# Value projections with 512 moving columns: four of six column groups of a three-block transformer stack

## The chip, the cores and the metric

One NeuronCore of one Trainium2 chip. The metric is the device time of one execution in microseconds, the median over runs; each execution takes some 2.2 ms. A core has a matrix engine (TensorE, PE in the profile; its weight loads are a row of their own, PEld), VectorE (DVE), ScalarE (ACT), GpSimd (POOL) and SyncE (SP), which here issues the weight loads from memory. The engines run their own lists of instructions in order and wait for each other by semaphores.

## What is computed

512 tokens of 1024 features go through a first block (a mixer that joins a four-head mLSTM and a gated convolution, then a feed-forward network) and two more layers (forgetting attention with 16 heads, then HGRN2 with 8 heads, each with its feed-forward network). Three projections matter here, those that make the values of the three mixers:

```
# first block                                   # second block, layer 0 (fox) and layer 1 (hgrn)
proj = u @ w_in                                 proj = einsum('bsd,de->bse', h, w_in)
qk_raw, v, o_pre, gates, glu = split(proj)      q, k, v, f_logit = split(proj)
qk = silu(causal_dwconv(qk_raw))                out = softmax(q k^T / 8 + c_q - c_k) v
q, k = split(qk)                                q, f_logit, i_val, g = split(proj)   # i_val: the values
h = mlstm_chunkwise(q, k, v, gates)             scores = q_t k_s decay(t, s);  o = scores v + ...
```

Each value projection is [512 tokens, 1024 features] times [1024, 1024]. All products are in float32 precision: an operand is split into a high and a low part, and a product is three matmuls (high by high, high by low, low by high), which accumulate in one PSUM bank.

## The kernel before

Activations lie feature-major in `U`, 8 blocks of [128 features, 512 tokens], each as a pair of high and low part. Weights come in units of 128 x 1024 numbers. Class `Weights` holds them in the order of use (the list `names` in `run`, L1683 to L1712): `load` (L145) has SP fetch a unit, `split` makes the high part on ACT (L155) and the low part on DVE (L157), and `take` hands a unit out. Three raw buffers and four of each part exist.

A product is made in one of two ways. `unit` (L440) makes 128 output features for all 512 tokens: the weights are the stationary operand, the tokens the 512 moving columns, 24 matmuls (8 k-blocks of three, L430 to L432). `unit_tok` (L452) makes values, which have to lie token-major: for each of four token blocks a 128 x 128 piece of `U` is stationary and 256 columns of weights move, 24 matmuls (L456 to L458) into one bank of half its width. So a `unit_tok` is 96 matmuls and takes two weight units at once. Both take their banks from `mm`, a ring of four; the side work has another ring of four, `ax`.

The order of PE and SP is the order of the code. Between pieces of the main stream stands `slot` (L387): it emits evacuations that are due (`post`, with a lag of one slot: a result is read out one slot after its last matmul) and then advances the side chains, generators that emit their next step at each slot (`ml_head`, `fox_pair`, `hgrn_head`, norms). A `unit` has a slot after k-blocks 2, 5 and 7, so after 9, 9 and 6 matmuls; a `unit_tok` has eight, one after every 12. ACT and DVE are ordered by a scheduler, which fills gaps of DVE with work of low priority (the 31-tap convolution, L838). `side(gen)` queues a chain; at most `maxside` run at a time, the next one starts when one ends, and `rate` is the number of steps per slot.

The three places:

- mLSTM (`first`, L897 to L907): for each head four `unit`s for q and k, each read out by `ev_qk` (ACT L879, three DVE operations L881, then the silu on ACT L883), then `unit_tok` for the head's 256 value columns, then `side(ml_head(h))`, then two `unit`s for the output gate. `ml_head` makes a broadcast of a gate row (PE L644 and L645), four exponentials of it (ACT L1036), the scores (PE L1045, two matmuls per token block, over the two halves of q and k), and at the end the product with the values (PE L1075).
- Forgetting attention (`fox`, L1320): a `unit_tok` before every other pair of heads, `fox_pair` as the side chain.
- HGRN2 (`hgrn`, L1548): a `unit_tok` after heads 0, 2 and 4 and one near the end; `hgrn_head` is the side chain. Its last steps are the product with the values (PE L1663 to L1667), the square (ACT L1670), the sums over features (PE L562), the power (POOL L567), the broadcast (PE L575), its copy (ACT L1677), two products on DVE (L1679, L1680) and the split into `O[h]` (ACT L599, DVE L600). `proj_out` (L1244) then multiplies all `O` with the output weights: `group` goes through the heads and emits slots until `O[k]` is there.

Of the kernel before, what the change touches and what calls it, by code (L numbers as in the profile page):

```python
# [42 lines left out]
def cols(v):  # L43
    """(..., C) with features along the last axis -> (128, ... * C/128)."""
    v = np.asarray(v)
    v = v.reshape(-1, v.shape[-1] // 128, 128)
    return np.ascontiguousarray(v.transpose(2, 0, 1)).reshape(128, -1)


def units(w, starts):  # L50
    """Column blocks of 128 of w (K, N): (len, 128, K)."""
# [5 lines left out]
def units_tok(w, start):  # L57
    """1024 columns of w (1024, N) as units of 256 columns and 4 k-blocks: (8, 128, 1024)."""
# [4 lines left out]
    return np.ascontiguousarray(np.concatenate(u))  # L63

# [5 lines left out]
def layout(inp):  # L70
# [30 lines left out]
    out["wv"] = units_tok(w, 2048)  # L101
# [16 lines left out]
    out["wfv"] = units_tok(w, 2048)  # L118
# [4 lines left out]
    out["whv"] = units_tok(w, 2048)  # L123
# [5 lines left out]
class Weights:  # L129
    """All weight units in the order of their use: loads and hi/lo splits run ahead of take()."""  # L130
# [30 lines left out]
    def take_blocks(self, tag):  # L161
        """A unit split into blocks of another tag."""
# [21 lines left out]
class Blocks:  # L184
    """A weight unit in two tiles."""
# [8 lines left out]
class Out:  # L194
    """The output of a phase: blocks y and the sums of their squares."""
# [14 lines left out]
class Norm:  # L210
    """x += rms(out) * g, then the blocks of x * gn, split; their norm r is applied later (box)."""
# [61 lines left out]
class ModNorm:  # L273
    """x += rms(out) * g, then the blocks of rms(x) * gain + shift, split."""
# [53 lines left out]
class Final:  # L328
    """x += rms(out) * g, stored."""
# [19 lines left out]
class Kernel:  # L349
# [39 lines left out]
    def slot(self):  # L389
        """Between two pieces of the main stream: due evacuations, side chains, fillers."""  # L390
# [15 lines left out]
    def fill(self, gen, late=1000000):  # L406
        """Work for idle engines."""
# [26 lines left out]
    def unit(self, U, evac, lag=1):  # L434
        """A block of 128 outputs, feature-major; evac(psum [128, T])."""
# [10 lines left out]
    def unit_tok(self, U, evac, lag=1, ax=0):  # L446
        """A block of 256 outputs, token-major; evac(tb, psum [128, 256])."""
# [15 lines left out]

    def group(self, n, get, evacs, kb=KB, ahead=1):
        """n units side by side, one k-block after the other as get(k) hands out its parts."""
# [11 lines left out]
    def group_halves(self, norm, evacs, extra=None, tag="Q"):  # L477
        """The first units of a phase, a half of the tokens after the other, as the norm hands out its blocks."""
# [24 lines left out]
    def tail(self, F, out, evac, nxt, done=4):  # L503
        """The last units of a phase, a half of the tokens after the other; each starts its part of the next norm."""
# [1002 lines left out]
    def hgrn(self, norm, nxt):  # L1507
# [42 lines left out]
        for h in range(6):  # L1550
# [3 lines left out]
            if h % 2 == 0:  # L1554
                self.unit_tok(U, ev_v(h // 2))
# [197 lines left out]
```

## Time and profile before

| what | value |
|---|---|
| three runs | 2204.05, 2207.32, 2210.89 us; median 2207.32 |
| profiled execution | span 2204.7 us from first to last instruction; its own time is not listed, only the span |
| granted TensorE clock, mean | 0.991 |
| PE busy | 2151.4 us, 98% of the span |
| PEld, DVE, ACT busy | 84%, 63%, 42% |
| weight traffic | 209 MB, 95 GB/s on average |

Busy PE does not mean PE at its peak: the ends of matmuls are modelled, and a matmul's record is longer than the distance to the next one's start. How fast PE goes is read from the distance between starts. Idle time of an engine that is not the bottleneck costs nothing.

### The profile page before, as it was taken

To read this page: it belongs to the slowest core of one execution; us is meant where nothing else is said; L and a number is where in the kernel's file an instruction comes from. 1 tells how busy PE (TensorE), PEld (TensorE's weight loads), DVE (VectorE), ACT (ScalarE), POOL (GpSimd) and SP (SyncE) were. 2 spreads that over 40 slices of the span, in tenths; PEclk is the share of its full clock that TensorE was granted. 3 is DMA by queue.
4 is the path that set the end of the run, shared out by engine and by line. 5 is a ranking of instruction groups with operands and counts; after the bars stand their busy time and mean duration, and the time that the engine had idled before them with its cause. 6 is when DMAs were issued, how large, how long until landed. Compare 5 with 4: busy or idle time off the path is not lost.

```text
span 2204.7 us, 30667 instructions
## 1 busy us (share of the span) xinstructions
PE 2151.4 (98%) x12224; PEld 1850.0 (84%) x12224; DVE 1395.6 (63%) x2391; ACT 917.8 (42%) x1485; POOL 52.8 (2%) x81
## 2 busy tenths in 40 slices
PE   7999999989999999999999999999999999999997
PEld 5788888888888889888898888888899889888887
DVE  4799999977455557755565243458787837434445
ACT  4434433555333334655543222236566544232221
POOL 0000000000000000000000000000000000000000
PEclk9999999999999999999999999999999999999999
DMA  8332224613422331212113223222211112232321
GB/s 293 106 134 77 68 68 134 230 58 127 141 95 89 105 94 56 71 58 67 59 58 117 100 94 100 93 89 88 77 49 58 49 58 96 87 105 89 103 91 62
DMA packets 67966, 209.01 MB, mean 95 GB/s; under 512 B 7664, under 2 KB 9840, under 8 KB 67824
## 3 DMA queue, kind: packets, MB, share of 16 engines
q1 hardware_dynamic: 67824, 207.06, 28.0%
q8 instruction: 96, 1.57, 0.3%
q14 instruction: 46, 0.38, 0.1%
HBM read 204.94 MB, written 2.10 MB: 94 GB/s over the span
## 4 chain that ended last, share of the span: by engine, by line
PE 71%; DVE 3%; ACT 2%; issue 1%; POOL 0%; DMA 0%; POOLq 0%; DVEq 0%; ACTq 0%
PE mm L430 19%; PE mm L431 19%; PE mm L432 19%; PE ax L1606 2%; PE mm L456 1%; PE mm L457 1%; PE mm L458 1%; PE ax L1435 1%; PE ax L1412 1%; DVE wl L157 1%; PE ax L562 1%; PE ax L432 1%; PE ax L430 1%; PE ax L431 1%; PE ax L1379 0%
## 5 line engine op out<-in xcount | busy, mean ns | idle before, releaser
L430 PE MATMUL mm<-U,wh 128*128 128x512 f32 (+1 forms) x1768 | 672.1, 380 | 4.1 <-ACT U L319 3.0
L432 PE MATMUL mm<-U,wl 128*128 128x512 f32 (+1 forms) x1768 | 657.8, 372 | 2.0 <-DVE wl L157 2.0
L431 PE MATMUL mm<-U,wh 128*128 128x512 f32 (+1 forms) x1768 | 657.4, 372 | 1.8 <-DVE U L320 1.8
L155 ACT CAST wh<-w 128x1024 fp32r<-128x1024 f32 (+1 forms) x325 | 335.6, 1035 | 748.0 <-PE mm L431 458.6
L157 DVE TENSOR_TENSOR wl<-w,wh 128x1024 fp32r<-128x1024 f32 (+1 forms) x325 | 389.8, 1202 | 208.5 <-ACT wh L155 185.0
L430 PEld LDWEIGHTS mm<-U,wh 128*128 128x128 f32 x1768 | 336.1, 190 | 65.0 <-issue 3.9
L432 PEld LDWEIGHTS mm<-U,wl 128*128 128x128 f32 x1768 | 335.4, 190 | 60.6 <-DVE wl L157 2.6
L431 PEld LDWEIGHTS mm<-U,wh 128*128 128x128 f32 x1768 | 335.9, 190 | 56.8 <-DVE U L320 2.3
L430 PE MATMUL mm<-H,wh 128*128 128x512 f32 (+1 forms) x868 | 309.2, 356 | 0.7 <-ACT H L599 0.7
L431 PE MATMUL mm<-H,wh 128*128 128x512 f32 (+1 forms) x868 | 306.5, 353 | 0.2 <-DVE H L600 0.2
L432 PE MATMUL mm<-H,wl 128*128 128x512 f32 (+1 forms) x868 | 306.5, 353 | 0.0
L430 PEld LDWEIGHTS mm<-H,wh 128*128 128x128 f32 x868 | 164.2, 189 | 23.3 <-ACT H L599 0.9
L432 PEld LDWEIGHTS mm<-H,wl 128*128 128x128 f32 x868 | 164.1, 189 | 22.8 <-DVE wl L157 0.2
L431 PEld LDWEIGHTS mm<-H,wh 128*128 128x128 f32 x868 | 164.2, 189 | 22.6 <-DVE H L600 0.5
L838 DVE SCALAR_TENSOR_TENSOR Y<-G,par,Y 128x505 f32<-128x505 f32 (+26 forms) x240 | 164.6, 729 | 0.5
L456 PE MATMUL mm<-wh,U 128*128 128x256 f32 x368 | 106.9, 291 | 0.0
L458 PE MATMUL mm<-wh,U 128*128 128x256 f32 x368 | 104.6, 284 | 0.0
L457 PE MATMUL mm<-wl,U 128*128 128x256 f32 x368 | 104.5, 284 | 0.0
L1203 DVE TENSOR_TENSOR Y<-Y,mm 128x512 f32<-128x512 f32 (+1 forms) x60 | 34.7, 580 | 106.6 <-PE mm L432 106.4
L1193 DVE TENSOR_TENSOR t<-t,mm 128x512 f32<-128x512 f32 x42 | 28.7, 686 | 102.0 <-PE mm L432 102.0
L1183 DVE TENSOR_TENSOR t<-mm,rb 128x512 f32<-128x512 f32 x42 | 29.0, 690 | 100.9 <-PE mm L432 100.9
L594 DVE TENSOR_TENSOR ss<-ss,t 128x256 f32<-128x256 f32 (+1 forms) x148 | 68.1, 466 | 29.3 <-ACT t L593 29.0
(364 smaller groups left out, 2747.7 us busy)
## 6 DMA issues: line engine op xcount, KB each, us to landing
w<-in_upa SPq DMA_DIRECT2D x44, 512.0 KB, 3.3
w<-in_upb SPq DMA_DIRECT2D x44, 512.0 KB, 3.2
w<-in_upc SPq DMA_DIRECT2D x44, 512.0 KB, 3.2
H<-in_ada SPq DMA_DIRECT2D x48, 256.0 KB, 6.0
w<-in_wglu SPq DMA_DIRECT2D x16, 512.0 KB, 3.8
w<-in_wqk SPq DMA_DIRECT2D x16, 512.0 KB, 3.3
U<-in_ada SPq DMA_DIRECT2D x32, 256.0 KB, 6.5
w<-in_wfqk SPq DMA_DIRECT2D x16, 512.0 KB, 3.3
```

Of the source, the lines that this page charges most:

```text
L155: nc.scalar.copy(wh, raw)
L157: k.V.tensor_sub(wl, raw, wh.bitcast(F32))
L430: mm(ps, lh, rh, start=start, stop=False)
L431: mm(ps, lh, rl, start=False, stop=False)
L432: mm(ps, ll, rh, start=False, stop=stop)
L456: mm(ps, lh, wh[:, k % 4], start=k == 0, stop=False)
L457: mm(ps, lh, wl[:, k % 4], start=False, stop=False)
L458: mm(ps, ll, wh[:, k % 4], start=False, stop=k == 7)
L594: self.V.tensor_add(ss, ss, sq)
L838: self.V.scalar_tensor_tensor(y[:, s:], G[j][:, :T - s], cvw[:, w:w + 1], y[:, s:], op0=ALU.mult, op1=ALU.add)
L1203: self.V.tensor_add(acc[m][:, c], acc[m][:, c], ps[:, c])
L1606: mm(ps[:, ts], W[:, ts], W[:, ts], start=True, stop=True)
```

## The change

A new function makes 512 value columns at a time. It takes four banks at once, one per token block, goes through the k-blocks outside (a weight unit is now 2 k-blocks of 512 columns) and through the token blocks inside, 6 matmuls of 512 moving columns each. After token blocks 0, 1 and 3 it has a slot.

```diff
+    def unit_wide(self, U, evac, lag=1):
+        mm = self.PE.matmul
+        pss = [self.mm() for _ in range(4)]
+        for u in range(4):
+            wh, wl = self.W.take(512)
+            for tb in range(4):
+                ts = slice(tb * 128, (tb + 1) * 128)
+                ps = pss[tb]
+                for k in (2 * u, 2 * u + 1):
+                    lh, ll = U[k][0][:, ts], U[k][1][:, ts]
+                    mm(ps, lh, wh[:, k % 2], start=k == 0, stop=False)
+                    mm(ps, lh, wl[:, k % 2], start=False, stop=False)
+                    mm(ps, ll, wh[:, k % 2], start=False, stop=k == 7)
+                if u == 3:
+                    self.post(lambda tb=tb, ps=ps: evac(tb, ps), lag)
+                if tb != 2:
+                    self.slot()
...
         def ev_v(h):
             def f(tb, ps):
-                nc.scalar.copy(V[tb][h // 2][:, (h % 2) * 256:(h % 2) * 256 + 256], ps)
+                nc.scalar.copy(V[tb][h // 2], ps)
+                if tb == 3:
+                    vdone.add(h // 2)
...
-            self.unit_tok(U, ev_v(h))
-            self.side(self.ml_head(h, qk, V, tho, H))
+            self.side(self.ml_head(h, qk, V, tho, H, vdone))
+            if h % 2 == 0:
+                self.unit_wide(U, ev_v(h))
...
         yield                                   # ml_head, after the scores
+        while h // 2 not in vdone:
+            yield
         num = []
...
         for p in range(8):                      # fox
-            if p % 2 == 0:
+            if p in (0, 2):
                 self.unit_tok(U, ev_v(p // 2), ax=2 if p == 0 else 0)
+            if p == 4:
+                self.unit_wide(U, ev_v(2))
...
             self.unit(U, ev_g(h))               # hgrn
-            if h % 2 == 0:
-                self.unit_tok(U, ev_v(h // 2))
+            if h == 0:
+                self.unit_wide(U, ev_v(0))
+            if h == 4:
+                self.unit_tok(U, ev_v(2))
```

The layout of the weights in memory and the order of the units in `names` follow; the read-outs in `fox` and `hgrn` take the width of what they get. So four groups of 512 columns are made in the new way (mLSTM at heads 0 and 2, attention at pair 4, HGRN2 at head 0), each in the place of two `unit_tok`, of which the second stood later: at the next head or two heads on. The mLSTM's side chain of a head is queued before the projection and no longer behind it. The last 256 columns of HGRN2 stay where they were. Docstrings and comments are dropped; lines move by 6 to 36.

PE at the first head of the mLSTM, from the broadcast of the gate row to the first scores. `rb` is the gate row, `Q` the q and k blocks, `wh` and `wl` the value weights (in the second list) and the output gate's weights (in the first).

```order
L644 MATMUL ax<-rb,identr 128x512
L645 MATMUL ax<-rb,identr 128x512
L430 MATMUL mm<-U,wh 128x512
L431 MATMUL mm<-U,wh 128x512
L432 MATMUL mm<-U,wl 128x512
L430 MATMUL mm<-U,wh 128x512
L431 MATMUL mm<-U,wh 128x512
L432 MATMUL mm<-U,wl 128x512
L430 MATMUL mm<-U,wh 128x512
L431 MATMUL mm<-U,wh 128x512
L432 MATMUL mm<-U,wl 128x512
L1045 MATMUL ax<-Q 128x512 x2
```

```order
L669 MATMUL ax<-rb,identr 128x512
L670 MATMUL ax<-rb,identr 128x512
L481 MATMUL mm<-wh,U 128x512
L482 MATMUL mm<-wl,U 128x512
L483 MATMUL mm<-wh,U 128x512
L481 MATMUL mm<-wh,U 128x512
L482 MATMUL mm<-wl,U 128x512
L483 MATMUL mm<-wh,U 128x512
L1073 MATMUL ax<-Q 128x512 x2
```

The first list begins 96 value matmuls and one piece of 9 behind the last q and k matmul; the second begins 6 matmuls behind it. At heads 1 and 3, where no projection is left in front, the second list begins 9 matmuls behind the last k matmul and has 9 in the middle.

ACT at the same place, from the read-out of the last k block (L879, now L904) on. L883, now L908, is the silu that makes k; L1036, now L1064, the exponentials; L895 copies values out; L155 splits weights.

```order
L879 ACTIVATE t<-mm,par 128x512
L895 COPY X<-mm 128x256 x2
L883 ACTIVATE Q<-t 128x512
L895 COPY X<-mm 128x256
L155 CAST wh<-w 128x1024
L895 COPY X<-mm 128x256
L155 CAST wh<-w 128x1024
L1036 ACT_TABLE_LOAD
L1036 ACTIVATE t<-ax,acol 128x512
```

```order
L904 ACTIVATE t<-mm,par 128x512
L1064 ACT_TABLE_LOAD
L1064 ACTIVATE t<-ax,acol 128x512
L1064 ACTIVATE t<-ax,acol 128x384
L1064 ACTIVATE t<-ax,acol 128x256
L1064 ACTIVATE t<-ax,acol 128x128
L908 ACT_TABLE_LOAD
L908 ACTIVATE Q<-t 128x512
L161 CAST wh<-w 128x1024 x3
```

The silu that makes the last k block now stands behind the exponentials, with a table load ahead of each; before, it stood ahead of them.

PE at the end of HGRN2, from the last product with values of the last head. `H` is `O`, `ones` gives the sums, `ident` the broadcast.

```order
L1666 MATMUL ax<-t,Y 128x256
L1667 MATMUL ax<-t,Y 128x256
L430 MATMUL mm<-H,wh 128x512
L431 MATMUL mm<-H,wh 128x512
L432 MATMUL mm<-H,wl 128x512
L430 MATMUL mm<-H,wh 128x512
L431 MATMUL mm<-H,wh 128x512
L432 MATMUL mm<-H,wl 128x512
L430 MATMUL mm<-H,wh 128x512
L431 MATMUL mm<-H,wh 128x512
L432 MATMUL mm<-H,wl 128x512
```

```order
L1702 MATMUL ax<-t,Y 128x256
L1703 MATMUL ax<-t,Y 128x256
L587 MATMUL ax<-ones,t 128x128 x4
L600 MATMUL ax<-ident,r 128x128 x4
L436 MATMUL mm<-H,wh 128x512
L437 MATMUL mm<-H,wh 128x512
L438 MATMUL mm<-H,wl 128x512
```

Before, 18 projection matmuls stood between the product with values and the sums, and 18 more between the broadcast and the 9 that read the last head's `O` (heads 3 to 6). Now all of these stand ahead of the product, and sums, broadcast and the last head's 9 matmuls follow each other with nothing between.

## Rows read from the trace of the kernel before

**Rows 1.** The page: its first line, and the busy time of the engines (us, share of the span, instructions).

```profile
span 2204.7 us, 30667 instructions
PE 2151.4 (98%) x12224; PEld 1850.0 (84%) x12224; DVE 1395.6 (63%) x2391; ACT 917.8 (42%) x1485; POOL 52.8 (2%) x81
```

**Rows 2.** Busy time by engine in stretches of the span (us; instructions in brackets; then clock, DMA share, GB/s): the q, k, value and gate projections of the first block, and the heads of HGRN2.

```profile
100.00:380.00 280.00, 280.00 (x1444) 231.85 (x1443) 269.80 (x411) 106.91 (x155) 16.02 (x20) 1.00 0.29 96
...
1540.00:1720.00 180.00, 178.93 (x1203) 163.28 (x1202) 139.01 (x321) 107.66 (x169) 7.96 (x5) 1.00 0.19 62
```

**Rows 3.** Timeline of PE (start, duration), first block: the first and the last of 23 matmuls of 512 columns in a row (22 distances), then the first and the last of 32 of 256 columns in a row (31 distances), from the first one of the first `unit_tok`.

```profile
144.84 0.39 PE L431 MATMUL mm<-U,wh 128*128 128x512 f32 x1
...
149.82 0.39 PE L432 MATMUL mm<-U,wl 128*128 128x512 f32 x1
156.17 0.28 PE L456 MATMUL mm<-wh,U 128*128 128x256 f32 x1
...
159.88 0.28 PE L457 MATMUL mm<-wl,U 128*128 128x256 f32 x1
```

**Rows 4.** Timeline of PE, head 0 of the mLSTM: the broadcast of the gate row and the matmul after it, the first scores (two matmuls, four records) and the matmul after them.

```profile
169.84 0.50 PE L644 MATMUL ax<-rb,identr 4*128 4x512 f32 x1
...
170.50 0.50 PE L430 MATMUL mm<-U,wh 128*128 128x512 f32 x1
...
172.68 1.88 PE L1045 MATMUL ax<-Q 128*128 128x512 f32 x4
173.99 0.79 PE L430 MATMUL mm<-U,wh 128*128 128x512 f32 x1
```

**Rows 5.** Timeline of ACT, head 0: read-out of the last k block, first value copy, the silus of q and k (the second belongs to the last k block), the exponentials, and a table load with the silu behind it.

```profile
157.63 0.76 ACT L879 ACTIVATE t<-mm,par 128x512 f32<-128x512 f32 x1
159.24 0.37 ACT L895 COPY X<-mm 128x256 f32<-128x256 f32 x1 [0.85 <-PE mm L458]
...
162.39 0.63 ACT L883 ACTIVATE Q<-t 128x512 f32<-128x512 f32 x1
...
169.22 1.28 ACT L1036 ACT_TABLE_LOAD   x1
170.61 1.78 ACT L1036 ACTIVATE t<-ax,acol 128x512 f32<-128x512 f32 x4
...
199.68 1.28 ACT L883 ACT_TABLE_LOAD   x1 [2.97 <-DVE v L1095]
200.97 0.63 ACT L883 ACTIVATE Q<-t 128x512 f32<-128x512 f32 x1
```

**Rows 6.** Timeline of ACT, heads 1, 2 and 3: for each the first value copy and the silu of the last k block.

```profile
218.08 0.37 ACT L895 COPY X<-mm 128x256 f32<-128x256 f32 x1 [1.75 <-PE mm L458]
219.95 0.63 ACT L883 ACTIVATE Q<-t 128x512 f32<-128x512 f32 x1 [1.50 <-DVE t L881]
...
275.14 0.37 ACT L895 COPY X<-mm 128x256 f32<-128x256 f32 x1 [0.85 <-PE mm L458]
...
278.29 0.64 ACT L883 ACTIVATE Q<-t 128x512 f32<-128x512 f32 x1
...
332.19 0.37 ACT L895 COPY X<-mm 128x256 f32<-128x256 f32 x1 [0.85 <-PE mm L458]
...
335.34 0.64 ACT L883 ACTIVATE Q<-t 128x512 f32<-128x512 f32 x1
```

**Rows 7.** Timeline of DVE, head 0: the last of the three operations on the last k block.

```profile
161.03 0.74 DVE L881 SCALAR_TENSOR_TENSOR t<-mm,par,t 128x509 f32<-128x509 f32 x1
```

**Rows 8.** Timeline of PE, end of HGRN2, last head: end of the product with values, the sums, the broadcast with PE's wait before it, the matmul after it, and the first one that reads the last head's `O`.

```profile
1779.27 0.59 PE L1667 MATMUL ax<-t,Y 128*128 128x256 f32 x2
...
1783.80 1.05 PE L562 MATMUL ax<-ones,t 128*128 128x128 f32 x8
1786.32 0.65 PE L575 MATMUL ax<-ident,r 128*128 128x128 f32 x4 [1.48 <-POOL r L567]
1786.73 0.48 PE L430 MATMUL mm<-H,wh 128*128 128x512 f32 x1
...
1790.91 0.39 PE L430 MATMUL mm<-H,wh 128*128 128x512 f32 x1
```

**Rows 9.** Timeline of ACT and DVE at the same place: the square after a product with values that ended at 1770.81, then the high and the low part of the last head's `O`.

```profile
1770.92 0.60 ACT L1670 ACTIVATE t<-ax 128x512 f32<-128x512 f32 x1 [2.47 <-PE ax L1667]
...
1789.20 0.62 ACT L599 CAST H<-t 128x512 fp32r<-128x512 f32 x1 [1.55 <-DVE t L1680]
...
1789.85 0.69 DVE L600 TENSOR_TENSOR H<-t,H 128x512 fp32r<-128x512 f32 x1 [0.69 <-ACT H L599]
```

**Rows 10.** Busy time in stretches, as in rows 2 (PE first, the clock third from the end): three pairs, each a wait of PE and what comes after it.

```profile
847.90:850.20 2.30, 0.14 (x2) 0.00 (x0) 1.72 (x5) 1.12 (x3) 0.00 (x0) 0.93 0.49 192
850.20:853.90 3.70, 3.63 (x19) 3.45 (x20) 2.89 (x9) 1.57 (x4) 0.69 (x1) 0.58 0.02 4
895.80:897.80 2.00, 0.06 (x3) 0.05 (x2) 1.94 (x3) 1.95 (x3) 0.00 (x0) 0.97 0.00 0
897.80:904.50 6.70, 6.70 (x25) 4.96 (x26) 3.13 (x4) 4.16 (x9) 0.00 (x0) 0.50 0.46 157
466.60:469.20 2.60, 0.45 (x2) 0.19 (x1) 2.50 (x8) 2.02 (x4) 0.00 (x0) 1.00 0.00 0
469.20:475.00 5.80, 5.76 (x48) 5.77 (x49) 2.17 (x6) 3.90 (x8) 0.58 (x1) 1.00 0.01 3
```

More of the change, by code (lines that the diff above doesn't have):

```diff
@@ L63, in units_tok, with units_wide @@
     return np.ascontiguousarray(np.concatenate(u))
+def units_wide(w, start):
+    blk = w[:, start:start + 512].reshape(4, 2, 128, 512)
+    return np.ascontiguousarray(blk.transpose(0, 2, 1, 3)).reshape(4, 128, 1024)
 def seq(start, n):
@@ L100, in layout @@
     out["wglu"] = units(w, [s for j in range(8) for s in (glu + 1024 + 128 * j, glu + 128 * j)])
-    out["wv"] = units_tok(w, 2048)
+    out["wv"] = np.concatenate([units_wide(w, 2048 + 512 * g) for g in range(2)])
     out["wqk"] = units(w, [s for h in range(NH) for b in (0, 1024) for s in seq(b + 256 * h, 2)])
@@ L117, in layout @@
     out["wff"] = np.ascontiguousarray(w[:, 3072:].reshape(KB, 128, FOXH).transpose(1, 0, 2)).reshape(128, 8 * FOXH)
-    out["wfv"] = units_tok(w, 2048)
+    out["wfv"] = np.concatenate([units_tok(w, 2048)[:4], units_wide(w, 2048 + 512)])
     out["wfqk"] = units(w, [s for p in range(8) for s in (128 * p, 1024 + 128 * p)])
@@ L122, in layout @@
     out["whf"] = units(w, seq(1024, 8))
-    out["whv"] = units_tok(w, 2048)
+    out["whv"] = np.concatenate([units_wide(w, 2048), units_tok(w, 2048)[4:]])
     out["whqg"] = units(w, [s for h in range(8) for s in (128 * h, 3072 + 128 * h)])
@@ L871, in first @@
         H = [None] * 8
-        qk, tho = {}, {}
+        qk, tho, vdone = {}, {}, set()
         def ev_qk(h, i):
@@ L1022, in gate_chain, with ml_head @@
         self.dump("gates", [Ar, mt])
-    def ml_head(self, h, qk, V, tho, H):
+    def ml_head(self, h, qk, V, tho, H, vdone):
         nc = self.nc
@@ L1305, in f @@
             def f(tb, ps):
-                nc.scalar.activation(V[tb][g // 2][:, (g % 2) * 256:(g % 2) * 256 + 256], ps, AF.Copy,
+                c = g % 2 * 256
+                nc.scalar.activation(V[tb][g // 2][:, c:c + ps.shape[1]], ps, AF.Copy,
                                      scale=box["r"][tb // 2][:, tb % 2:tb % 2 + 1])
@@ L1541, in f @@
                     V[tb][g // 2] = self.blk("Y")
-                nc.scalar.activation(V[tb][g // 2][:, (g % 2) * 256:(g % 2) * 256 + 256], ps, AF.Copy,
+                c = g % 2 * 256
+                nc.scalar.activation(V[tb][g // 2][:, c:c + ps.shape[1]], ps, AF.Copy,
                                      scale=box["r"][tb // 2][:, tb % 2:tb % 2 + 1])
@@ L1690, in run @@
         for h in range(NH):
-            names += some("wqk", 4 * h, 4 * h + 4) + some("wv", 2 * h, 2 * h + 2) + some("wo", 2 * h, 2 * h + 2)
+            names += some("wqk", 4 * h, 4 * h + 4)
+            if h % 2 == 0:
+                names += some("wv", 2 * h, 2 * h + 4)
+            names += some("wo", 2 * h, 2 * h + 2)
         names += every("woh") + every("woy")
@@ L1701, in run @@
         for p in range(8):
-            if p % 2 == 0:
-                names += some("wfv", p, p + 2)
+            if p % 2 == 0 and p < 6:
+                names += some("wfv", p, p + (4 if p == 4 else 2))
             if p >= 2:
@@ L1708, in run @@
             names += some("whqg", 2 * h, 2 * h + 2)
-            if h % 2 == 0:
-                names += some("whv", h, h + 2)
+            if h in (0, 4):
+                names += some("whv", h, h + (4 if h == 0 else 2))
         names += some("whqg", 12, 13) + some("whqg", 14, 15) + some("whv", 6, 8) + some("whqg", 13, 14) + some("whqg", 15, 16)
```

## Prediction

> **What bounds the kernel now.** I read the page first: PE works in 98% of the span, DVE in 63%, ACT in 42% [rows 1]. Then the stretches in which the change sits: in 280 us of projections of the first block PE is not idle at all, while DVE is busy 96% of the time; in the heads of HGRN2 PE misses 1.1 us of 180 [rows 2]. So the end moves by what PE gains or loses, and every new wait of PE counts in full. How fast PE goes is in the distance of starts: 22 distances of 512-column matmuls take 4.98 us, 226.4 ns each; 31 of 256 columns take 3.71 us, 119.7 ns each [rows 3]. Last I followed, from PE's new order, what its first scores and the end of HGRN2 wait for, in the timelines of ACT, DVE and PE.
>
> **The change part by part.** *Matmuls.* Four groups of 512 columns: 2 x 96 matmuls of 256 columns each become 96 of 512. 768 x 119.7 ns = 91.9 us become 384 x 226.4 ns = 86.9 us: a gain of 5.0 us [rows 3]. Bound below: 0 if the new ones don't keep that distance; above: nothing more, the distance is measured. The number of weight loads halves too, but each runs beside a matmul.
>
> The rule that speaks against this gain is in the Trainium skill, "TensorE: Matmul & The Clock Gate", section "Back-to-back issue gap": the columns over 2.4 per ns, plus some 2.5 ns. By it two matmuls of 256 cost 218 ns and one of 512 costs 216, and the gain would be an estimated 1.0 us instead of 5.0. The trace has some 11 ns more for each [rows 3], and so twice that where there are two; I go by the rows.
>
> *The scores of the mLSTM.* Call T the moment in which the last k matmul of a head is done and the next piece begins. Before, the head's chain began behind the value projection, some 15 us later, and nothing was awaited. Now the broadcast stands 6 matmuls behind T and the scores 6 further: 1.36 + 0.66 + 1.36 us, and the second matmul of the scores, which reads the last k block, 0.65 later (the broadcast takes 169.84 to 170.50, the two matmuls of scores 172.68 to 173.99 [rows 4]). PE is there at T + 4.0. When is that block ready? Before: T is 156.17 [rows 3], the silu ends at 163.02 [rows 5], T + 6.85, since DVE's last operation on it ends at 161.77 only [rows 7], between convolution taps; their order on DVE is not changed there. That alone makes PE wait 2.8 us. In the new ACT order two table loads (1.28 each) and four exponentials (1.78) also stand ahead of the silu: read-out done at 158.39, T + 2.2; then 1.28, 1.78 and 1.28 end at T + 6.6, and the silu of 0.63 at T + 7.2 [rows 5]. Wait at head 0: 3.2 us. For the other heads T lies 3.1 us ahead of the first value copy, as at head 0 [rows 3, 5], which gives silus at T + 5.6, 6.9 and 6.9 before [rows 6]; I add the same 0.35. Head 2 has the wide projection too: 3.2 us. Heads 1 and 3 have pieces of 9 matmuls, so PE arrives at 2.04 + 0.66 + 2.04 + 0.65 = T + 5.4 and waits 0.6 and 1.8. Sum: 8.8 us lost. Bounds: 5 us (ACT without the detour at all heads, 2.8 + 0.2 + 2.9 + 1.5 would be 7.4, less some convolution that gives way) and 12 us (0.8 more per head where DVE's taps crowd). Behind the waiting matmul on PE stands everything else, so nothing covers it.
>
> *Banks.* The wide projection takes its four banks at once; the last is the one of the last k block, needed at T + 5.4 at the earliest with the side work. It is free at 161.77, T + 5.6 [rows 7], and PE stands in the wait above by then: 0. Value copies are fewer and wider, off the path: 0. Weight units are used at the same pace, one per 5.4 us instead of two per 11.5, and are no longer held in pairs: 0, and SP's order only follows.
>
> *End of HGRN2.* The group of 512 columns and the projection that vanishes at head 2 leave four slots fewer, so the chains end later against the main stream. Before, the last head's product with values ended at 1779.86; then came 18 matmuls, the sums, a wait of 1.48 us for the power, the broadcast, and 18 more matmuls, so that the first one that needs the last `O` came at 1790.91 [rows 8], when high and low part were ready (1789.82 and 1790.54 [rows 9]). Now nothing lies between. The square begins 0.1 us after the product and takes 0.6 [rows 9]: 0.75 us of waiting before the sums. The wait for the power is there as before. After the broadcast PE would go on at 1786.73, but the high part comes 3.1 us later, and the low part, for the second matmul, holds it up by 0.45 more [rows 8, 9]. Sum: 4.3 us lost, with bounds of 2 (if an earlier wait of PE in the same phase, 1.1 us up to 1720 [rows 2], goes away with the wider spacing) and 5.
>
> *Forgetting attention and the rest of HGRN2.* The side work meets pieces of 1.36 and 2.7 us instead of 1.44, elsewhere of 2.04: gains and losses of tenths at both. I take 0, bounds -1.5 and +2.
>
> *Clock.* Three new waits are of 3 us and more (heads 0 and 2, end of HGRN2). In the trace PE's clock fell to the lower of its two levels, 1.2 GHz, after waits of some 2 us: after the one at 847.9 the next 3.7 us ran at 0.58, 1.55 us lost; after the one at 895.8, 6.7 us at 0.50, 3.35 us lost; after the one at 466.6, in two pieces, it did not fall [rows 10]. I take 1.55 for each of the three, 4.7 us (the middle value, and the three events' mean is 1.6), with bounds of 0 and 10.
>
> *Sum.* -5.0 + 8.8 + 0 + 4.3 + 0 + 4.7 = +12.8 us, against the profiled span of 2204.7. The median of the runs, 2207.32, lies 2.6 above that span; I put the sum on the median: 2220.
>
> **The rivals.** (1) *The clock holds.* One of the three waits in the rows did not bring it down. Then the sum is +8.1: 2215. (2) *The waits vanish, and only the distance counts.* It decides at T + 4.0: if DVE let its three operations on the last k block go one behind the other, without the two taps and the weight split between them, they would end 2.5 us sooner, and the exponentials on ACT would find the gap. Then only the gain and the end of HGRN2 are left, -5.0 + 4.3 + 1.55 = +0.9: 2208; with the end hidden too, 2202.3. Against it: the order of DVE at that place is the same as before, and the detour on ACT is fixed in its order; it would have to be so at four heads. Up to 1.4 us might come back later where PE waits for others. (3) *The clock falls hard*, 3.35 us at all five waits: +24.9, 2232. (4) *The switch of tables costs more than its load.* Two more switches stand in each head's path; with 1.38 us more each, four heads wait 11 us longer: 2231. In the rows the silu starts 0.01 us after the end of a table load [rows 5], so it has little chance. The rule behind it is in the Trainium skill, "ScalarE: Activation LUTs", section "What ACT_TABLE_LOAD costs": 1283 ns for the load and some 1380 ns for a drain; this trace agrees with the first and shows nothing of the second.
>
> **How the numbers follow.** A run of this kernel can be told from no change where it differs by about 0.3%, 6.6 us: under 2200.7 is faster, over 2213.9 slower. Chances: the forecast, with the clock falling as in the middle row, 0.52, nearly all of it slower; rival 1 0.20, of which a quarter, with the lower bounds of the waits, is within 0.3%; rival 2 0.20, 0.15 of it within 0.3% and 0.05 faster, where another phase gains too; rival 3 0.05 and rival 4 0.03. So slower 0.75, within 0.3% 0.20, faster 0.05. The range is 2206 to 2230: it takes in the forecast with the bounds of its terms, rival 1 and the upper half of rival 2, and leaves out the rest of that and rivals 3 and 4, some 0.18.
>
> **What would show it.** In the new profile, distances of 226 ns in the wide projection and 92 us of 256-column value matmuls less. In the waits of PE, a row of scores (L1073) for ACT's silu (L908), four times, 0.6 to 3.2 us, 9 in all; today there is none. At the end of HGRN2 a wait of the sums (L587) for the square, and one of `H` (L624, L625) of 3 us. The clock below 1 shortly after. PE without idle time in the first block's projections would refute the second term, and with it the forecast; a long wait for a bank of `mm` or for weights would mean that I looked in the wrong place.

## Result: 20 us slower, and where the time went

The changed kernel takes 2227.34 us (median of 4 runs, 2226.68 to 2228.10), against 2207.52 us of the kernel before in the same comparison (4 runs, 2204.05 to 2210.89). The ratio is 1.0086, with a 95% interval of 1.0074 to 1.0098. The forecast was 2220 us, slower by 12.8; the measured difference is +19.8 us. The profiled execution took 2228.1 us, its span is 2226.4.

The first look is at the page of the changed kernel, its first line and the busy times (us, share, instructions), as in [rows 1]:

```profile
span 2226.4 us, 29878 instructions
PE 2157.5 (97%) x11840; PEld 1835.7 (82%) x11840; DVE 1392.8 (63%) x2391; ACT 921.2 (41%) x1473; POOL 56.5 (3%) x81
```

384 matmuls are gone, and yet PE is busy for 6.1 us more. Busy time also grows when the clock falls, since each matmul then lasts longer. So I split every stage of both traces in three: time in which PE had no matmul, time lost to the clock (1 minus the granted clock, times the busy time of PE, over each stretch of one clock), and the rest. The stages begin with the first matmul that reads a stage's operands; all of it is worked out from the matmul and clock records of the two traces, in us, and the last column is the change's difference (no matmul / clock / rest).

| stage | before | after | difference |
|---|---|---|---|
| projections of the first block | 335.6 | 344.6 | +9.0 (+9.0 / +1.7 / -1.7) |
| its output projections | 109.2 | 112.6 | +3.4 (+1.8 / +1.7 / -0.1) |
| start of its feed-forward | 99.3 | 100.6 | +1.2 (0.0 / +1.4 / -0.2) |
| attention, with its output | 275.4 | 275.0 | -0.4 (+0.6 / -0.2 / -0.7) |
| HGRN2, heads | 277.9 | 276.3 | -1.7 (-0.3 / +2.9 / -4.2) |
| HGRN2, output projection | 55.8 | 65.9 | +10.2 (+3.5 / +3.6 / +3.0) |
| last feed-forward | 369.3 | 368.7 | -0.6 (+0.6 / -1.5 / +0.2) |

The two feed-forward stages in between are the same within 0.2 us. All stages together are 21.3 us longer: +15.2 without a matmul, +9.7 for the clock, -3.7 for the rest (the rest of HGRN2's two rows is one number, -1.2: side work moved from the first into the second). To the 21.6 us between the two spans it takes 0.6 more at the start and 0.3 less at the end. Each trace is one execution; the medians differ by 19.8, so some 2 us of what the two traces show are not in the medians.

**The waits.** Some of the longest waits of PE in the changed kernel (engine, line, what it waited for: us in all, times, the longest). The second row (scores) and those of the read-out L942 and the square L1706 had no counterpart before; the first was 17.3 us, the third 6.8, the row of `H` 0.7:

```profile
PE ax L587 <- DVE ss L619: 18.0, 8, 10.2
PE ax L1073 <- ACT Q L908: 9.0, 4, 3.1
PE ax L600 <- POOL r L592: 8.1, 8, 1.5
PE mm L436 <- ACT H L624: 3.5, 2, 2.8
...
PE mm L436 <- ACT Q L942: 1.7, 1, 1.7
...
PE ax L587 <- ACT t L1706: 0.7, 1, 0.7
```

The read-out L942 is late in the first block's output projections; here PE waits for it:

```profile
425.71 0.39 PE L436 MATMUL mm<-G,wh 128*128 128x256 f32 x1 [1.67 <-ACT Q L942]
```

On ACT it stands behind two splits of weights (L624, L161), and the first of these had waited for its load:

```profile
423.61 0.62 ACT L624 CAST H<-w 128x512 fp32r<-128x512 f32 x1 [4.59 <-DMA w<-in_woy]
...
425.08 0.58 ACT L942 COPY Q<-mm 128x512 f32<-128x512 f32 x1
```

**Head 0 of the mLSTM**, timeline of PE (start, duration; what PE waited for in brackets). It answers to [rows 3, 4]. T, the end of the last k matmul's turn, is 156.69:

```profile
156.46 0.39 PE L438 MATMUL mm<-U,wl 128*128 128x512 f32 x1
156.69 0.39 PE L481 MATMUL mm<-wh,U 128*128 128x512 f32 x1
...
160.29 1.02 PE L1073 MATMUL ax<-Q 128*128 128x512 f32 x2
164.34 2.08 PE L1073 MATMUL ax<-Q 128*128 128x512 f32 x2 [3.02 <-ACT Q L908]
```

ACT at the same place, which answers to [rows 5]:

```profile
158.92 1.28 ACT L1064 ACT_TABLE_LOAD   x1
160.22 1.78 ACT L1064 ACTIVATE t<-ax,acol 128x512 f32<-128x512 f32 x4
162.36 1.28 ACT L908 ACT_TABLE_LOAD   x1 [0.36 <-DVE t L906]
163.65 0.63 ACT L908 ACTIVATE Q<-t 128x512 f32<-128x512 f32 x1
```

And the last of DVE's three operations on this k block, as in [rows 7]:

```profile
161.54 0.74 DVE L906 SCALAR_TENSOR_TENSOR t<-mm,par,t 128x509 f32<-128x509 f32 x1
```

DVE's last operation ends at 162.28, T + 5.6, as before the change. The second table load only begins then, and so the silu ends at T + 7.6 instead of T + 7.2.

**End of HGRN2**, timeline of PE from the last product with values on; it answers to [rows 8]:

```profile
1802.41 0.59 PE L1703 MATMUL ax<-t,Y 128*128 128x256 f32 x2
1803.69 1.16 PE L587 MATMUL ax<-ones,t 128*128 128x128 f32 x8 [0.69 <-ACT t L1706]
1806.33 1.12 PE L600 MATMUL ax<-ident,r 128*128 128x128 f32 x4 [1.48 <-POOL r L592]
1810.28 0.79 PE L436 MATMUL mm<-H,wh 128*128 128x512 f32 x1 [2.83 <-ACT H L624]
```

ACT there, the square and the high part of the last head's `O`, as in [rows 9]:

```profile
1803.04 0.60 ACT L1706 ACTIVATE t<-ax 128x512 f32<-128x512 f32 x1 [5.39 <-PE ax L1703]
...
1809.61 0.62 ACT L624 CAST H<-t 128x512 fp32r<-128x512 f32 x1 [1.54 <-DVE t L1716]
```

**The clock.** Busy time in stretches of the changed kernel, in the columns of [rows 2, 10] (PE first, the granted clock third from the end): a wait and what follows it, at head 0, head 2, the start of HGRN2, and its end; then the two stretches of [rows 2].

```profile
161.30:164.30 3.00, 0.01 (x1) 0.00 (x0) 3.00 (x6) 2.61 (x5) 1.77 (x4) 1.00 0.11 44
164.30:167.50 3.20, 3.16 (x6) 1.86 (x7) 3.20 (x6) 0.00 (x0) 0.00 (x0) 0.51 0.00 0
282.20:285.30 3.10, 0.03 (x1) 0.00 (x0) 3.10 (x6) 2.60 (x5) 3.10 (x4) 1.00 0.18 70
285.30:289.00 3.70, 3.63 (x14) 2.67 (x15) 3.70 (x6) 0.02 (x1) 3.38 (x1) 1.00 0.00 0
...
1502.40:1506.30 3.90, 2.32 (x16) 1.94 (x14) 3.90 (x10) 3.43 (x8) 0.00 (x0) 0.93 0.44 146
1506.30:1512.50 6.20, 5.13 (x24) 4.84 (x23) 5.30 (x13) 2.94 (x7) 0.00 (x0) 0.50 0.59 181
1802.60:1805.90 3.30, 1.56 (x10) 0.97 (x8) 0.16 (x1) 0.60 (x1) 0.64 (x1) 1.00 0.00 0
1805.90:1816.20 10.30, 7.04 (x17) 5.13 (x18) 4.05 (x5) 5.39 (x9) 0.37 (x1) 0.51 0.10 34
100.00:380.00 280.00, 271.05 (x1212) 215.39 (x1211) 260.58 (x401) 103.05 (x140) 20.63 (x20) 0.99 0.27 88
1550.00:1730.00 180.00, 177.56 (x1088) 157.50 (x1087) 139.19 (x320) 109.18 (x165) 5.05 (x4) 1.00 0.20 65
```

Two waits of 3 us, the same code at two heads: behind the first PE ran at half speed, behind the second it did not. The traces of runs 4 and 5 below, which have both waits too, show the same: a fall at head 0 and none at head 2.

**The distance of the new matmuls**, PE, head 0, the first and the last of 28 in a row (27 distances, 6.12 us, 226.7 ns each; [rows 3] had 226.4):

```profile
175.75 0.39 PE L481 MATMUL mm<-wh,U 128*128 128x512 f32 x1
...
181.87 0.39 PE L481 MATMUL mm<-wh,U 128*128 128x512 f32 x1
```

### The profile page after: what moved, and what is told of

It reads as the page before. It is cut to its first block, busy times and chain, and to the rows that moved or that the text cites. A ratio compares the mean times of both kernels' runs of the same rounds, so it can differ in the third digit from the quotient of the medians.

```text
span 2226.4 us, 29878 instructions
## 1 busy us (share of the span) xinstructions
PE 2157.5 (97%) x11840; PEld 1835.7 (82%) x11840; DVE 1392.8 (63%) x2391; ACT 921.2 (41%) x1473; POOL 56.5 (3%) x81
## 4 chain that ended last, share of the span: by engine, by line
PE 69%; DVE 4%; ACT 2%; issue 1%; POOL 0%; DMA 0%; POOLq 0%; DVEq 0%; ACTq 0%
PE mm L436 19%; PE mm L437 19%; PE mm L438 19%; PE ax L1642 2%; PE ax L1468 1%; PE ax L587 1%; PE ax L1445 1%; DVE wl L163 1%; PE ax L438 1%; PE mm L481 1%; PE mm L482 1%; PE mm L483 1%; PE ax L436 1%; PE ax L437 1%; PE ax L1412 0%
## 5 line engine op out<-in xcount | busy, mean ns | idle before, releaser
L161 ACT CAST wh<-w 128x1024 fp32r<-128x1024 f32 (+1 forms) x325 | 335.7, 1035 | 781.9 <-PE mm L437 445.2
L863 DVE SCALAR_TENSOR_TENSOR Y<-G,par,Y 128x501 f32<-128x501 f32 (+27 forms) x240 | 163.5, 726 | 0.1
L592 POOL TENSOR_TENSOR r<-v,neghalf 128x2 f32<-128x2 f32 (+1 forms) x36 | 33.7, 937 | 1704.2 <-DVE v L609 1575.2
L624 ACT CAST H<-t 128x512 fp32r<-128x512 f32 x82 | 50.7, 619 | 57.8 <-DVE t L1223 48.4
L625 DVE TENSOR_TENSOR H<-t,H 128x512 fp32r<-128x512 f32 x82 | 56.2, 685 | 12.3 <-ACT H L624 12.3
```

What stands on the lines that cost most here:

```text
L161: nc.scalar.copy(wh, raw)
L592: self.nc.gpsimd.tensor_tensor(r, v, self.neghalf[:, 0:v.shape[1]], op=ALU.pow)
L624: nc.scalar.copy(hi, src)
L625: self.V.tensor_sub(lo, src, hi.bitcast(F32))
L863: self.V.scalar_tensor_tensor(y[:, s:], G[j][:, :T - s], cvw[:, w:w + 1], y[:, s:], op0=ALU.mult, op1=ALU.add)
```

## Experiments

Each was timed in five rounds, beside the kernel before on the same chip; the ratio is to that kernel, with its 95% interval. The median of the kernel before lay between 2207.85 and 2208.94 there, and at 2207.52 in the comparison above, so a difference between runs of different groups is uncertain by about a microsecond. Stage numbers are worked out as in the table above, from one traced execution of each.

**1. Scores three slots later.** In the changed kernel:

```diff
         while (h, 3) not in qk:
             yield
+        for _ in range(3):
+            yield
```

> The changed kernel, with the mLSTM head's side chain held back by three slots before its broadcast (about 6 us at heads 0 and 2, 5.4 us at heads 1 and 3). Theory of the prediction: the four waits of the scores for the silu of the last k block (9.0 us in the trace of the change) go, the silu stands ahead of the exponentials on ACT again, and the fall of the clock behind head 0's wait (1.7 us) goes too: 2227.3 - 9.0 - 1.7 = 2216.6; other falls may come or go by 1.7 each. Rival A (the wide projection itself is what costs, by its banks or its pace): the waits move to another matmul and the time stays at 2225 to 2229. Rival B (falls of the clock are chance, not tied to waits): 2218.3, with PE's clock still falling at the place.

Measured: 2225.14 us, ratio 1.0078 (1.0064 to 1.0092), 2 us below the changed kernel and not 11. The waits for the silu are gone, all four. In their place PE waits for the bank of the last k block at heads 0 and 2, 3.5 us in all; here is head 0 on PE, in the wide projection:

```profile
161.41 0.39 PE L483 MATMUL mm<-wh,U 128*128 128x512 f32 x1
163.31 0.47 PE L481 MATMUL mm<-wh,U 128*128 128x512 f32 x1 [1.50 <-DVE t L906]
```

And DVE's last operation on that k block in this kernel:

```profile
162.42 0.74 DVE L906 SCALAR_TENSOR_TENSOR t<-mm,par,t 128x509 f32<-128x509 f32 x1
```

The same DVE operation that made the silu late frees the bank late, at T + 5.6 (T is 157.56 here). The four banks at once do cost something here. In the changed kernel this was covered by the wait for the silu, and in part by the chain's own broadcast and scores: without them in front, PE reached this matmul at T + 4.1 and not at the T + 5.4 of the prediction. And the last head's chain, now later, kept the output projection waiting 3.4 us for its high part. Both theories held in part: the waits were the early chain's, but holding the chain back let two others out.

**2. The kernel before, chain first.** All projections 256 columns wide:

```diff
+            self.side(self.ml_head(h, qk, V, tho, H, vdone))
             self.unit_tok(U, ev_v(h))
-            self.side(self.ml_head(h, qk, V, tho, H))
...
+        while h not in vdone:       # ml_head, ahead of the product with the values
+            yield
```

> The kernel before, all value projections 256 columns wide, with only the queueing changed: the mLSTM head's side chain is queued ahead of its value projection, and its product with the values waits for them. Theory of the prediction: it is the early chain and not the width that makes the waits. PE is at the second matmul of the scores at T + 1.44 + 0.66 + 1.44 + 0.65 = T + 4.2 at all four heads, the silu ends at T + 7.2, 5.9, 7.2 and 7.2, so about 3 us at heads 0, 2 and 3 and 1.7 at head 1: 10.7 us of waits, 1.7 of clock for each of two or three falls: 2207.5 + 10.7 + 3.4 to 5.1 = 2222 to 2223. Rival A (the width, its banks): no wait, 2207.5.

Measured: 2226.24 us, ratio 1.0082 (1.0068 to 1.0096). The row of the scores in PE's waits of this kernel:

```profile
PE ax L1047 <- ACT Q L883: 11.8, 4, 3.5
```

Forecast 10.7. So the wait does not need the width: queueing the chain ahead of the projection, at 256 columns, makes it too, and costs almost as much as the whole change. The clock lost 6.3 us more in that stage than before, not 3.4 to 5.1.

**3. Waits filled.** The changed kernel with useless matmuls in three places:

```diff
+                if d == 0 and sb == 0 and h % 2 == 0:
+                    self.warm(4, k[0][:, 0:128], q[0])      # scores
...
+        if h == 7:                      # hgrn_head, ahead of the sums
+            self.warm(3, O[0][0][:, 0:128], O[0][0])
...
+        if h == 7:                      # ahead of the broadcast
+            self.warm(6, O[0][0][:, 0:128], O[0][0])
...
+        if h == 7:                      # behind it
+            self.warm(12, O[0][0][:, 0:128], O[0][0])
```

> The changed kernel with useless matmuls in the waits: four between the two matmuls of the first scores of heads 0 and 2 (0.65 us each), and at the end of HGRN2 three ahead of the last head's sums, six between sums and broadcast and twelve behind the broadcast (0.23 us each, 4.8 us). They write a bank that nobody reads. No wait for another engine becomes shorter; only PE is not idle. Theory of the prediction (the clock falls because PE stood still): the fall at head 0 (3.4 us at half speed, 1.7 us lost) and the one at the end of HGRN2 (10.2 us, 5.1 lost) go, 2227.3 - 6.8 = 2220.5, perhaps less 1 or 2 for work that overlapped badly. Rival B (the falls are chance, or come from something else than idle PE): they stay, 2227 to 2229.

Measured: 2220.66 us, ratio 1.0057 (1.0045 to 1.0070), 6.7 us below the changed kernel. Busy time and clock at head 0 and at the end of HGRN2, the two places which ran at 0.51 in the changed kernel (columns as in [rows 2]):

```profile
164.00:168.00 4.00, 4.00 (x14) 2.30 (x13) 3.79 (x6) 1.31 (x2) 0.11 (x1) 1.00 0.00 0
1800.00:1812.00 12.00, 11.59 (x51) 8.80 (x50) 5.87 (x8) 7.16 (x11) 0.85 (x1) 1.00 0.14 45
```

With PE at work through the waits it went on hardly sooner behind them, and the clock stayed up. But only part of the 6.7 us is from there: the output stage of HGRN2 became 3.0 us shorter, the first projections 0.6 (the useless matmuls ran on past the wait), while 4.0 in the trace came from the first block's output projections, where the read-out (L942) was on time and the clock did not fall. The total agreed better than its parts.

**4. Faster steps at the end of HGRN2.**

```diff
+        self.rate = 1.5
         self.unit_tok(U, ev_v(3))
```

> The changed kernel with 1.5 instead of 1.1 steps per slot from the last value projection of HGRN2 on, so that the last head's product with the values stands 27 output matmuls into the output projection (as before the change) instead of 63, its sums at 36 and its broadcast at 45, with 18 matmuls left ahead of the first one that needs its result. Theory of the prediction: the waits for the square and for the high part (0.7 + 2.8 us) go, and the fall behind them (10.2 us at half speed) shrinks to what the kernel before had, one of 3.4 us or none: 2227.3 - 3.5 - 3.4 to 5.1 = 2218.7 to 2220.4. Rival A (the end of HGRN2 is bounded by the chain's engines, not by its slots): faster steps make other waits in the chain, 2225 to 2229.

Measured: 2220.87 us, ratio 1.0062 (1.0049 to 1.0075), 6.5 us below the changed kernel, half a microsecond above the forecast. The output stage has 0.6 us without a matmul instead of 5.0 and nothing lost to the clock; the heads have 1.9 us more without a matmul. That steps which follow closer wait more is the likely reason, not a shown one. So the end of HGRN2 was a matter of slots, as the second term of the loss had it.

**5. The mLSTM's part alone**, attention and HGRN2 as before.

> The mLSTM's part of the change alone: wide projections at heads 0 and 2, the chains queued ahead; attention and HGRN2 as in the kernel before. From the stages of the two traces: waits of the scores 9.0, a read-out awaited in the output projection 1.7 (with other waits 3.4 in all), falls of the clock 1.7 to 5, matmul time -2.5 to -3.4: 2207.5 + 12 to 15 = 2219.5 to 2222.5. By the prediction's terms (-2.5 + 8.8 + 3.1) 2216.9. If the parts did not add (a gain of the mLSTM's that the end of HGRN2 undoes, or the other way), it would be outside 2215 to 2223.

Measured: 2221.95 us, ratio 1.0060 (1.0047 to 1.0073; the five runs lie between 2216.96 and 2223.45). Its profiled execution has the same row of waits as the changed kernel, to the digit:

```profile
PE ax L1073 <- ACT Q L908: 9.0, 4, 3.1
```

So 14 of the 20 us are the mLSTM's. The traced execution is the fastest of the five, 2216.96 us, and its trace is 10.7 us longer than the one of before; what the others have more of stands in no trace. The read-out L942 is awaited for 0.5 us in this trace, 1.7 in the changed kernel's; it is not a fixed price of the part.

**6. Gate unit first.** The changed kernel, with one gate unit between a head's q and k and its chain:

```diff
+            o = [[0, 1], [2, 3], [4], [5, 6, 7]][h]
+            self.unit(U, ev_o(o[0]))
             self.side(self.ml_head(h, qk, V, tho, H, vdone))
             if h % 2 == 0:
                 self.unit_wide(U, ev_v(h))
-            for i in range(2):
-                self.unit(U, ev_o(2 * h + i))
+            for i in o[1:]:
+                self.unit(U, ev_o(i))
...
```

> The changed kernel with the mLSTM's gate units in another order: one unit for the output gate stands between the q and k units of a head and its side chain (and its wide projection), and head 3 keeps two more gate units behind its chain. So the broadcast comes 6.8 to 7.5 us behind the last k matmul, and the wide projection reaches its last bank 5.4 us later. Theory: the waits of the scores (9.0 us), of the bank (3.5 us, seen only where the scores were held back) and of the output projection (1.7 us behind a read-out on ACT, 3.4 us for the high part of the last heads where the chain was held back) are all gone, and with them two falls of the clock (164.1 and 427.0 us of the changed kernel, 1.7 each): 2227.3 - 9.0 - 1.7 - 3.4 = 2213.2. Rival A (the wide projection itself costs): waits come back at its banks or weights, 2220 or more. Rival B (falls are chance): 2216.6.

Measured: 2217.28 us, ratio 1.0043 (1.0031 to 1.0056), 4.1 us above the forecast. The first block's projections take 333.0 us, 2.6 less than before: no wait, and the matmul gain of two groups (2.5 forecast) is all there. It does not last: the next stage is 5.8 us longer than before. PE in the first output projection:

```profile
369.18 0.39 PE L438 MATMUL mm<-H,wl 128*128 128x512 f32 x1
373.71 2.08 PE L1155 MATMUL ax<-ss,ones 128*128 128x512 f32 x2 [4.14 <-DVE ss L871]
```

And what it waited for, on DVE:

```profile
372.97 0.69 DVE L871 TENSOR_TENSOR ss<-ss,Y 128x512 f32<-128x512 f32 x1
```

L871 is the last sum over the 31-tap convolution, the work of low priority that fills DVE. In the kernel before it ended 0.14 us ahead of the matmul that needs it. PE of before:

```profile
372.11 0.61 PE L1123 MATMUL ax<-ss,ones 128*128 128x512 f32 x1
```

DVE of before:

```profile
371.28 0.69 DVE L846 TENSOR_TENSOR ss<-ss,Y 128x512 f32<-128x512 f32 x1
```

DVE and PE both were at their limit in the first block. In the changed kernel this cannot be seen: while PE waits for the silu, DVE goes on with the taps, and the sum ends at 361.8.

**7. Gate unit first and faster steps.**

> The same, and 1.5 steps per slot from the last value projection of HGRN2 on, as in the run that changed that alone (2220.9, 6.5 below the changed kernel). Theory: all waits that the change brought are gone, and what is left is the shorter matmul time: the kernel before less 5.0 us, plus one fall of 3.4 us that comes at the start of HGRN2 in some kernels: 2202.5 to 2206; by the runs' own differences 2213.2 - 6.5 = 2206.7. Rival A (512 columns gain nothing, as the rule of columns and a small gap would have it): 2206.5 to 2210.

Measured: 2213.33 us, ratio 1.0023 (1.0014 to 1.0032), above all forecasts. Against the kernel before, the wait for the convolution (4.1 us) with its fall of the clock (2.4 us) stands in the first block, and a fall of 2.8 us at the start of HGRN2.

**8. The convolution's sum later**: six steps instead of three ahead of it.

> The kernel with the gate unit first and faster steps at the end of HGRN2 (2213.3), with the sum over the convolution's features placed three slots later in the first block's output projection (behind 60 of its matmuls instead of 36, 5.4 us of matmuls). Theory: in the first block DVE is a bound of its own; its convolution ends at 372 to 374 us whatever PE does, and PE's gain there had become a wait of 4.1 us for it, with a fall of the clock (6.8 us at half speed, 3.4 lost). With other work put in front, both go: 2213.3 - 4.1 - 3.4 = 2205.8. Rival A (the products with the convolution are late by as much further on): the wait moves to the matmuls that read them, 2211 to 2214. Rival B (falls are chance): 2209.

Measured: 2214.15 us, ratio 1.0026 (1.0016 to 1.0037), just above rival A. The wait for the convolution is gone, but DVE's other work is late in its place; from PE's waits in the block's output projections (358.41 to 473.62 us):

```profile
PE ax L587 <- DVE mod L719: 2.1, 1, 2.1
...
PE mm L438 <- DVE wl L163: 1.4, 2, 0.9
...
PE mm L436 <- DVE Q L971: 0.9, 1, 0.9
```

In run 7 only the second of these is there, with 0.2 us.

**9. Sixteen taps less**, of 240, in the kernel of 7:

```diff
-            for s in range(1, CVK):
+            for s in range(3, CVK):
```

> The kernel with the gate unit first and faster steps (2213.3), with 16 of the convolution's 240 taps on DVE left out (the second and third tap of each of the 8 blocks, some 0.7 us each, 11 us of DVE); PE's order is the same. Theory: in the first block DVE is a second bound, 0.1 us behind PE in the kernel before, and turned PE's gain of 2.5 us there into a wait of 4.1 us for the convolution, with a fall of the clock of 3.4 us behind it. With less on DVE both go: 2213.3 - 4.1 - 3.4 = 2205.8, and the first block alone ends 2 to 3 us ahead of the kernel before. Rival A (PE is the only bound there, DVE has slack): 2213.3. Rival B (the wait goes, falls are chance): 2209.2.

Measured: 2207.16 us beside 2208.94 of the kernel before, ratio 0.9992 (0.9983 to 1.0001), 6.2 us below the run with all taps (7.1, if each is taken against the kernel before in its own rounds). The first block's projections and output take 442.3 us together, where the kernel before has 444.8: 2.6 us less, the gain of two groups, at last at the end of the block. Without the taps DVE holds PE back no longer, as the second bound has it. The total stayed 1.4 us above the forecast; the fall that went had cost 2.4 us in run 7's trace, not 3.4. HGRN2's fall (2.9 us) stands in both. The kernel before without these taps was not run.

**10. Attention and HGRN2 wide, faster steps, the mLSTM as before.**

> The mLSTM as before; the wide projections of attention and HGRN2, with 1.5 steps per slot at the end of HGRN2. Theory: no wait is new, only matmul time is saved, 2.5 us: 2205.0, or 2208.4 where the clock falls at the start of HGRN2 for 6.8 us, as in most kernels of this study but not in the one before. If 512 columns gained only the estimate of the rule of columns and a small gap, 0.5 us, 2207 to 2210.4. If the faster steps cost as much in HGRN2's heads as they save at its end: 2211 to 2214.

Measured: 2209.97 us, ratio 1.0010 (1.0001 to 1.0019), above both forecasts of the theory. The rest, without waits and clock, is 0.7 us less in attention and 1.0 less in HGRN2: 1.7 of the 2.5 forecast. Over all stages, 2.6 us more are without a matmul than before (30.9 against 28.3) and 3.7 us more are lost to the clock (17.5 against 13.8).

**11 and 12. The waits of attention filled**, in the kernel before, and in that of 7.

> The kernel before, nothing moved, with useless matmuls of 128 columns in two waits of its own in forgetting attention: ten ahead of the sums of the first half (wait of 2.2 us at 848) and nine ahead of the first scores (1.9 us at 896). They write into a bank that is written anew afterwards. Theory (the clock falls because PE stands still): the falls behind these two waits (3.4 and 6.8 us at half speed) go: 2207.5 - 1.7 - 3.4 = 2202.4. Rival B (the falls have another cause): 2207.5, or a little more for work that does not fit the wait.

> Gate unit first, faster steps at the end of HGRN2, and the two waits of attention filled. If the gains add, 5.1 us below the run without the filling: 2197.5 to 2201.6, below both kernels. If the falls are chance, as without the filling, 2202.5 to 2207.

Measured: 2212.63 us (ratio 1.0017, 1.0008 to 1.0026) and 2215.05 us (1.0026, 1.0017 to 1.0035). Both missed their aim: in the first one's trace the useless matmuls ran at 859.8 and at 908.7 us, beside the waits, which still had 2.23 and 2.02 us; they cost their 19 x 0.22 = 4.2 us. On what a filled wait does here they say nothing. In both traces the fall behind the second wait lasted 3.4 us instead of the 6.8 of all the others; why stays open, as the useless matmuls next to it began only when it was over. The first gave something else. At the start of HGRN2, where nothing was edited, its waits are those of the kernel before (1.4, 1.0 and 0.6 us on the same three operands), and yet:

```profile
1494.00:1499.00 5.00, 2.04 (x12) 1.45 (x11) 5.00 (x13) 3.12 (x8) 0.00 (x0) 0.82 0.58 193
1499.00:1504.00 5.00, 5.00 (x25) 5.00 (x25) 3.56 (x8) 2.44 (x6) 0.00 (x0) 0.50 0.52 170
```

The kernel before ran at 1.00 there:

```profile
1489.00:1494.00 5.00, 2.03 (x13) 1.45 (x13) 5.00 (x13) 3.15 (x7) 0.00 (x0) 1.00 0.58 197
1494.00:1500.00 6.00, 6.00 (x52) 5.95 (x51) 5.57 (x15) 3.04 (x8) 0.69 (x1) 1.00 0.56 185
```

Of the 14 traces, ten have this fall; the four without are the kernel before, the runs 1, 2 and 5. Run 1 has HGRN2 as the change makes it, this one as before, so the change alone does not decide it. But it goes with the change: nine of the ten traces with the changed HGRN2 have the fall, and one of the four with HGRN2 as before. What in the change makes it likelier was not tested. The clock also differs between executions of one kernel: in the rounds of run 9, six of 15 executions of the kernel before had a mean clock of 0.989 and took 2209.33 to 2210.79 us, the other nine had 0.990 to 0.992 and took 2207.52 to 2209.14. So a fall of 2 or 3 us in a single trace may not be in the median.

## Why the prediction was right in kind and short in size

**Matmul distance (-5.0): nearly right, -3.7 in the changed kernel.** The distance is 226.7 ns, as the rows had it. Where waits did not hide it, a stage's rest fell by 2.6 (first block, run 6), 0.7 (attention) and 1.0 (HGRN2, both run 10), 4.3 together. The rule of the Trainium skill, "TensorE: Matmul & The Clock Gate", section "Back-to-back issue gap", by which it was an estimated 1.0, does not fit these runs; the page gives it for an isolated matmul.

**Scores of the mLSTM (+8.8): 9.0.** By head 3.0, 1.1, 3.1 and 1.7, forecast 3.2, 0.6, 3.2, 1.8. Run 2 shows that the place of the chain makes them, run 1 that they go with it. That the sum fits so well has luck in it, since two errors inside cancelled: PE came at T + 4.6 and not at T + 4.0, and the silu ended at T + 7.6 and not at T + 7.2, since its table load started only behind DVE's last operation.

**Banks (0): right in the changed kernel, but only as cover.** I had named the wait and the side work that hide them; run 1 took both away, and 3.5 us came out.

**End of HGRN2 (+4.3): 3.5.** 0.69 for the square (0.75), 2.83 for the high part (3.1); the low part's 0.45 was not seen. Run 4 shows that the missing slots are the cause.

**Attention and the rest of HGRN2 (0): right for waits**, +0.6 and -0.3; the fall at the start of HGRN2 is counted with the clock.

**Clock (+4.7): this is the term that was too small: 9.7.** At the three places that I named it took 1.7, 0 and 3.6, 5.3 in all, against 3 x 1.55. What I left out are falls elsewhere: 1.7 and 1.4 in the two stages behind the mLSTM, 2.9 at the start of HGRN2 and 0.2 in a feed-forward stage, less 1.5 and 0.2 that did not come again. One of these has a new wait in front of it, the read-out L942, 1.7 us late on ACT behind weights that had waited 4.59 us for their load; that wait had no term either. For the others the waits are those of before or shorter. Run 3 shows that the clock stays up when PE works through a wait; which of the unfilled waits brings it down I cannot say from these runs.

**Sum.** Waits 15.2 where 13.1 were forecast, clock 9.7 where 4.7, matmuls and the rest -3.7 where -5.0: 21.3 us in the two traces and 19.8 in the medians, where 12.8 were forecast. The time lies 2.7 us inside the upper end of the range; the waits and the sign were foreseen, the full size was not.

**Rivals.** (1) *The clock holds*: refuted. (2) *The waits vanish*: refuted, DVE's operations ended at T + 5.6 as in the rows. (3) *The clock falls hard* is nearer to the time (2232) than the forecast, but not for its reason: the five waits lost 5.3 us to the clock, not 16.75. (4) *A switch of tables costs more than its load*: refuted, the load ends at 163.64 and the silu starts at 163.65.

**What the prediction did not see** is that the gain in the first block could not be had by taking the waits away. I noted DVE's 96% there and went by PE alone. Runs 6, 8 and 9 show DVE as a second bound: its convolution was done 0.14 us before PE needed it, and in run 6, without the waits, the gain of 2.6 us became a wait of 4.1 for the convolution.

No version with the whole computation beat the kernel before; the nearest is run 10.

## What to carry to other kernels

Where an engine's work of low priority ends just when the busiest engine needs it, a gain on the busiest engine alone can be worth nothing: look for the consumer of that work and its slack before counting matmuls. A projection that stands between a block's making and its use is cover; if a change moves the consumer ahead of it, price the whole chain that makes the block, on all engines, from the moment of the last matmul. Price a new wait with a fall of the clock behind it, and leave as much again in the range for falls at places that the change does not touch.

## What the runs showed of the hardware

Like waits in like places bring PE's clock down in some traces and not in others. With HGRN2 as before, the same three waits at its start (1.4, 1.0 and 0.6 us) brought a fall in run 11 and none in the kernel before. In the changed kernel 3.0 us at head 0 did and 3.1 at head 2 did not, and so it was in the two other traces with these waits. At the lower level, 1.2 GHz, 512-column matmuls of the changed kernel stood 0.43 us apart behind head 0's wait (starts at 166.63, 167.06 and 167.49), against 0.227 otherwise. With useless matmuls in the wait the granted clock stayed at 1.00 in the two filled places that had run at 0.51. The table load ahead of the last k block's silu started only when the operand of that silu was there (162.36, behind DVE's 162.28), so it added its 1.28 us to the path even where ACT had been idle before it (0.36 us). Not every table load waits so: the one ahead of the exponentials in the kernel before started at 169.22, before the broadcast that they read (169.84) [rows 4, 5].
